# A SwiGLU down projection by seven products: sums of the activations formed by accumulating transfers instead of by VectorE

## The chip, the cores and the metric

The kernel runs on one core of a Trainium2 chip. The metric is the device time of one execution in microseconds (us). Its core has TensorE (PE in the profile; PEld is its weight load), VectorE (DVE), ScalarE (ACT), GpSimd (POOL) and SyncE (SP), which work side by side and wait for each other through semaphores, and 16 DMA engines that carry all transfers. A transfer is issued by an engine's queue, here SP's or GpSimd's; one that adds to what lies at its destination is issued by GpSimd.

## The reference

A layer of a streaming encoder over 512 positions of width 1024, in float32. The part that matters is its end, the feed-forward network, with 2816 inner channels:

```
h2 = rms_norm(x, norm_ffn[l])
act = silu(h2 @ w_ffn_gate) * (h2 @ w_ffn_up)
x = x + act @ w_ffn_down
```

## The kernel before, in words

Every matmul operand is split into a high part, rounded to the format that TensorE takes (float32r), and a low part, the rest; a product is three matmuls (high-high, low by high, high by low). Weights are split as they come: ScalarE copies the raw tile to the high part (`whd` in the down projection), VectorE subtracts to get the low part (`wld`). The weight tiles have three buffers.

The feed-forward network is computed in steps c = 0 to 10, each of which leaves a block of 256 channels, `act0` to `act10`, each 128 x 2 x 512 (its last axis is the position). `finish_act` ends a step: it adds what TensorE summed, multiplies the gate half and the up half by `rb2` (the inverse root mean square of each position), applies SiLU to the gate half and multiplies. It is called for tx and for ty, the tiles of a step's two halves of 128 channels, each with gate and up half side by side.

The down projection does `act0` directly (L1587 to L1605) and the other ten blocks by a seven-product scheme (Winograd's form of Strassen's), which replaces eight block products by seven on sums of blocks. The activations are cut in 2 x 2: inner half i (act1 to act5, act6 to act10) by position half j. A block (i, j) is named by `ablk` in three parts kh of two, two and one acts. The products run in the order

```
DORDER = ("11", "12", "S1", "S2", "S3", "S4", "22")
```

and take as activation operands: block (0,0); block (1,0); T1 = (0,0) - (0,1); T2 = -T1 - (1,1); T3 = (1,1) - (0,1); block (1,1); T4 = -T2 - (1,0). VectorE forms T1, T2 and T4 in place of block (0,0) and T3 in place of (0,1) (`in_place`, L1570), five instructions each. `split_d2` splits an operand: ScalarE writes the high part (L1400), VectorE the low part (L1401), into tiles `Bd` + the product's name + kh + h or l. So `BdS10h` is the high part of the first third of T1.

The weights of each product lie in five sets n = 0 to 4 of 512 KB. Raw sets of product 11 are `dw110` to `dw114`, of product 21 `dw210` to `dw214`; sums of weights for S1, S2 and S3 are formed in them by accumulating transfers from DRAM on GpSimd's queue (`dadd`, L1537), each issued when the set has been split. Sets of products 12 and 22 come on SP's queue into three raw buffers, `dr120` to `dr124` and `dr220` to `dr224`; the fourth load waits until the first set has been split. Each product is done for two output halves q; with `USE` the five sets follow each other once: sets 0, 1 and half of set 2 for q = 0, the other half and sets 3, 4 for q = 1. The profile leaves numbers out of names, so `whd<-dr` is any high part of a set of product 12 or 22, and `act<-act` any of the in-place sums.

What stands where between the products is written out by hand: the table `LATER` lists, for each product, calls that prepare later operands, and after each of a product's six pieces two (q = 0) or one (q = 1) of them are recorded. The order on each engine then follows from priorities of a scheduling layer, except where `keep_in_program_order` holds it. An engine does its instructions in that order, and a waiting one holds up all behind it on the same engine.

Of the kernel before, what the change touches and what calls it, by code (L numbers as in the profile page):

```python
# [8 lines left out]
F32 = mybir.dt.float32  # L9
F32R = mybir.dt.float32r  # L10
BF16 = mybir.dt.bfloat16
AF = mybir.ActivationFunctionType
ALU = mybir.AluOpType
# [18 lines left out]
H = S // 2  # L32
# [34 lines left out]
def layer_kernel(ctx: ExitStack, tc: tile.TileContext, x, xt, vecs, w_in, w_qkv7, w_gate7, w_pool, w_rg, w_ig,  # L67
                 w_branch, w_br7, w_out, w_fd, w_gu7, w_fd7, out):
    nc = tc.nc
    act = nc.scalar.activation  # L70
    dve = nc.vector
# [12 lines left out]
    def b4(shape, name, tag="b", dt=F32):  # L84
        bufs = {"w": NAW, "t": NAT, "b": NAB}[tag]
        return pools["ap0"].tile([P] + shape, dt, tag=tag, name=name, bufs=bufs)
# [317 lines left out]
    with ExitStack() as first:  # L404
# [394 lines left out]
        for t in VKQ:  # L799
            ps = {}  # L800
            r = {}
# [15 lines left out]
            for nm in ORDER:  # L817
                if nm in ("11", "12", "S1", "22"):
                    bank(nm)
                dst = {"S2": "11", "S3": "11", "S4": "S1"}.get(nm, nm)  # L820
# [28 lines left out]
        for cc in range(2):  # L849
            tx, ty = b4([2, S], f"gx{cc}"), b4([2, S], f"gy{cc}")  # L850
# [3 lines left out]
            Y = pb.tile([P, 2, S], F32, tag="mm", name=f"ps_gy{cc}")  # L854
            X = pb.tile([P, 2, S], F32, tag="mm", name=f"ps_gx{cc}")
# [8 lines left out]
            for nm in ORDER:  # L864
                ps, half, first_, t, ts_, src, ss = plan[nm]
# [314 lines left out]
    with ExitStack() as third:  # L1180
# [42 lines left out]
        for u, nm in BORDER:  # L1223
# [3 lines left out]
            ps = bank[u, z]  # L1227
            ah = weights("b7", u, nm)
            b = BH[nm]
            for w in range(2):  # L1230
                o = ps[:, w, half * H:(half + 1) * H]
# [4 lines left out]
            if sn is not None:  # L1236
                if (u, sn) not in snaps:
                    snaps[u, sn] = ap2.tile([P, 2, S], F32, tag="t", name=f"bt{u}{sn}")
                with tc.high_priority(EARLY):
                    act(snaps[u, sn][:, :, ts_], ps[:, :, hi], AF.Copy,  # L1240
                        scale=-1.0 if sn and (u, sn) in gated else 1.0)
# [10 lines left out]
    with ExitStack() as ffn:  # L1252
        gp = ffn.enter_context(tc.tile_pool(name="gp", bufs=GBUFS))

        def g4(shape, name, dt=F32):

            return gp.tile([P] + shape, dt, tag="g", name=name)

        def small(name, bufs=1, tag=None, dt=F32):
            return gp.tile([P, S], dt, tag=tag or name, name=name, bufs=bufs)  # L1260
# [3 lines left out]
        act(onesr, ones, AF.Copy)  # L1264
        sqsum = small("sqsum")
        rb2 = small("rb2")

        x1p = {}
        x1 = []

        def rms2():
            sh = small("sqh", 2, "sq2", F32R)
            sl = small("sql", 2, "sq2", F32R)
            act(sh, sqsum, AF.Copy)
            dve.tensor_tensor(sl, sqsum, sh.bitcast(F32), ALU.subtract)
            ps = fp.tile([P, 2, S], F32, tag="mm", name="ps_rms2")[:, 0, :]
            for n, t in enumerate((sh, sl)):
                tc.keep_in_program_order(nc.tensor.matmul(ps, onesr, t, start=n == 0, stop=n == 1))
            ms = small("ms2", 2, "sq2")
            t = small("rst2", 2, "sq2")  # L1280
            dve.tensor_scalar(ms, ps, 1.0 / D, EPS, ALU.mult, ALU.add)
            tc.keep_in_program_order(nc.scalar.preload_act_table_set("natural_log_exp_and_others"))
            act(t, ms, AF.Ln)
            act(t, t, AF.Exp, scale=-0.5)
            dve.tensor_tensor(rb2, t, t, ALU.mult)
            dve.tensor_tensor(rb2, rb2, ms, ALU.mult)
            dve.tensor_scalar(rb2, rb2, -0.5, 1.5, ALU.mult, ALU.add)
            dve.tensor_tensor(rb2, rb2, t, ALU.mult)

# [95 lines left out]
        def ablk(i, kh, j):  # L1387
            return [acts[1 + 5 * i + 2 * kh + n][:, :, j * H:(j + 1) * H] for n in range(2 - kh // 2)]

        def split_d2(nm, kh, i, j):  # L1390

            pin = tc.keep_in_program_order if nm not in ("11", "12") else lambda i: None
            if kh < 2:
                h, l = g4([4, H], f"Bd{nm}{kh}h", F32R), g4([4, H], f"Bd{nm}{kh}l", F32R)
            else:
                t = g4([2, 2, H], f"Bd{nm}{kh}", F32R)
                h, l = t[:, 0], t[:, 1]
            for n, src in enumerate(ablk(i, kh, j)):
                ns = slice(2 * n, 2 * n + 2)
                act(h[:, ns, :], src, AF.Copy)  # L1400
                pin(dve.tensor_tensor(l[:, ns, :], src, h[:, ns, :].bitcast(F32), ALU.subtract))  # L1401
            DB[nm, kh] = h, l

        def finish_act(t, ps, a, sign):

            dve.tensor_tensor(t, t, ps, ALU.add)
            for w in range(2):
                dve.tensor_tensor(t[:, w, :], t[:, w, :], rb2, ALU.mult)
            act(t[:, 0, :], t[:, 0, :], AF.Silu, scale=sign)
            if sign > 0:  # L1410
                dve.tensor_tensor(a, t[:, 0, :], t[:, 1, :], ALU.mult)
            else:
                dve.scalar_tensor_tensor(a, t[:, 1, :], sign, t[:, 0, :], ALU.mult, ALU.mult)


        PRE = ("S2", "S4", "22")

        def seven(n):
            c, nm = steps[n]
            lo, hi = slice(0, H), slice(H, S)  # L1420
            if nm == "11":
                acts.append(g4([2, S], f"act{c}"))
                T[c] = g4([2, S], f"tx{c}"), g4([2, S], f"ty{c}")
                Z[c] = [fp.tile([P, 2, S], F32, tag="mm", name=f"ps_{z}{c}") for z in "yx"]
            (tx, ty), (Y, X), a = T[c], Z[c], acts[c]
            make_a(n + 3)
            if c == 0:
                ps, kh = (Y, X)[CH[nm]], KH[nm]
                w = A.pop((c, nm))
                for j in range(2):  # L1430
                    product(w, B[0, f"{kh + 1}{j + 1}"], ps, j, kh == j == 0, kh == 1)
                for f in SPREAD[nm]:
                    f()
                if kh:
                    t = (tx, ty)[CH[nm]]
                    for w in range(2):
                        dve.tensor_tensor(t[:, w, :], ps[:, w, :], rb2, ALU.mult)
                    act(t[:, 0, :], t[:, 0, :], AF.Silu)
                    dve.tensor_tensor(a[:, CH[nm], :], t[:, 0, :], t[:, 1, :], ALU.mult)
                return  # L1440

            ps, half, first, t, ts_ = {"11": (Y, 1, True, tx, lo),
                                       "12": (X, 0, True, None, None),
                                       "S1": (X, 1, False, ty, hi),
                                       "S2": (Y, 1, False, tx, hi),
                                       "S4": (X, 1, False, None, None),
                                       "22": (Y, 0, False, None, None),
                                       "S3": (Y, 1, False, ty, lo)}[nm]
            product(A.pop((c, nm)), B[0, WITH[nm]], ps, half, first, True)
            if t is not None:  # L1450
                with tc.high_priority(EARLY):
                    act(t[:, :, ts_], ps[:, :, hi], AF.Copy)
            if (c, nm) == (1, "S1"):
                split_b("T3", "T3")
            if c == DOWN - 1 and nm == "S2":
                ah.extend(g4([2, S], "a" + p_, F32R) for p_ in "hl")
                act(ah[0], acts[0], AF.Copy)
                dve.tensor_tensor(ah[1], acts[0], ah[0].bitcast(F32), ALU.subtract)
            if c == DOWN - 1 and nm in PRE:
                split_d2("11", PRE.index(nm), 0, 0)  # L1460
            if nm == "S4":
                finish_act(tx, X, a[:, 0, :], 1.0)
            if nm == "S3":
                finish_act(ty, Y, a[:, 1, :], -1.0)

        T, Z, ah = {}, {}, []

# [2 lines left out]
        for c in range(4):  # L1470
# [13 lines left out]
            for j in range(2):  # L1484
# [3 lines left out]
                t = x1p[c // 2, j][:, c % 2, :]  # L1488
# [15 lines left out]
        for n in range(len(steps)):  # L1504
            seven(n)
# [6 lines left out]
        for m in range(4):  # L1512
            t = fp.tile([P, 2, S], F32, tag="mm", name=f"ps_d{m}")
# [54 lines left out]
        def in_place(dst, sign, op, other):  # L1568
            return [lambda kh=kh: [tc.keep_in_program_order(
                dve.scalar_tensor_tensor(t, t, sign, o, ALU.mult, op)) for t, o in zip(ablk(dst[0], kh, dst[1]), ablk(other[0], kh, other[1]))]  # L1570
                    for kh in range(3)]

        def both(nm, i, j):
            return [lambda kh=kh: split_d2(nm, kh, i, j) for kh in range(3)]
# [4 lines left out]
                   lambda: [dload("21", n, DX) for n in range(5)],  # L1579
                   lambda: [dadd("22", n, DX) for n in range(5)]] + both("12", 1, 0)[:1])  # L1580

        LATER = {"11": both("12", 1, 0)[1:] + in_place((0, 0), 1.0, ALU.subtract, (0, 1)) + both("S1", 0, 0),
                 "12": in_place((0, 0), -1.0, ALU.subtract, (1, 1)) + both("S2", 0, 0),
                 "S1": in_place((0, 1), -1.0, ALU.add, (1, 1)) + both("S3", 0, 1),
                 "S2": both("S4", 1, 1) + in_place((0, 0), -1.0, ALU.subtract, (1, 0)),
                 "S3": both("22", 0, 0)}

        for e in range(2):
# [48 lines left out]
        for nm in DORDER:  # L1637
            z, half, first, adds = plan[nm]
            todo = LATER.get(nm, [])
            n0 = dsets.index((nm, 0))  # L1640
            for q in range(2):
                if (nm, q) == ("22", 1):

                    make_d(len(dsets))
                    for w, ps in enumerate((XY[1, "y"], XY[0, "x"])):
# [3 lines left out]
                        t = x1p[q, 1][:, ws, lo]  # L1649
# [67 lines left out]
```

## Time and profile before

| | us |
|---|---|
| median of 3 runs | 900.3 |
| lowest, highest | 899.79, 902.87 |
| the profiled execution's own time | 900.52 |
| its span in the trace | 898.7 |
| TensorE busy | 891.1 |
| VectorE busy | 736.7 |
| ScalarE busy | 532.9 |
| GpSimd busy | 106.7 |

The span runs from the first to the last instruction; the execution's own time has 1.8 us around it.  A timeline row gives start and duration in us, engine, line, operation, what is written and read, shapes, and in brackets the idle time before it with what ended it. A row of transfers gives count, KB of each and the median time from issue to landing. The down projection by seven products begins at about 795 us of the span and ends with it.

### The profile page before, as it was taken

The page shows a single profiled execution, that of the slowest core. Times are in us where ns is not written, and L with a number is a line of the kernel's source. Part 1 is how long each engine was busy: PE and PEld are TensorE (multiplying, and loading weights), DVE is VectorE, ACT ScalarE, POOL GpSimd, SP SyncE. Part 2 cuts the span into 40 slices and gives each one's busy share as a digit, 9 for nine tenths or more (in the row PEclk, how much of TensorE's full clock was granted, in tenths as well). Part 3 has the DMA queues.
Part 4 walks back from the last instruction along what each step waited for, and adds up shares of the span by engine and source line. Part 5 has one row for each costly group of instructions (what it writes and reads, how often), then busy time and mean ns, then how long its engine had stood idle before and what let it go on. Part 6 is the DMA issues. An engine that isn't in the chain of part 4 may idle for free.

```text
span 898.7 us, 14578 instructions
## 1 busy us (share of the span) xinstructions
PE 891.1 (99%) x5731; PEld 802.4 (89%) x5731; DVE 736.7 (82%) x937; ACT 532.9 (59%) x747; POOL 106.7 (12%) x150
## 2 busy tenths in 40 slices
PE   9999999999999999999999999999999999998998
PEld 6888778888899888888888988999999999998998
DVE  7897897988786599967887685798888888998974
ACT  7554989556856556555664545655555555654642
POOL 1010002232332101000001100000010100121200
PEclk9999999999999999999999999999999999999999
DMA  9485347798582786634635864836666676887913
GB/s 342 141 309 150 114 132 210 220 299 244 179 262 71 234 234 192 218 118 145 214 93 154 190 179 164 258 81 174 169 148 176 162 169 201 211 210 205 196 39 117
DMA packets 83620, 164.59 MB, mean 183 GB/s; under 512 B 7904, under 2 KB 48864, under 8 KB 83552
## 3 DMA queue, kind: packets, MB, share of 16 engines
q1 hardware_dynamic: 68000, 107.29, 35.9%
q0 software_dynamic: 15408, 56.11, 28.2%
q8 instruction: 45, 0.74, 0.3%
q10 hardware_dynamic: 144, 0.26, 0.1%
q14 instruction: 23, 0.19, 0.1%
HBM read 143.19 MB, written 18.87 MB: 180 GB/s over the span
## 4 chain that ended last, share of the span: by engine, by line
PE 93%; DVE 3%; ACT 2%; DMA 1%; issue 1%; DVEq 0%; ACTq 0%; SPq 0%
PE ps_y L283 13%; PE ps_x L283 10%; PE ps_q L794 7%; PE ps_dy L1633 5%; PE ps_dx L1633 4%; PE ps_br L274 3%; PE ps_br L275 3%; PE ps_br L276 3%; PE ps_bY L1234 2%; PE ps_gy L283 2%; PE ps_gate L697 2%; PE ps_gate L276 2%; PE ps_bX L1234 2%; PE ps_gx L283 2%; PE ps_gate L274 2%; PE ps_gate L275 2%
## 5 line engine op out<-in xcount | busy, mean ns | idle before, releaser
L110 ACT ACTIVATE whi<-raw 128x1024 fp32r<-128x1024 f32 x61 | 64.6, 1059 | 73.3 <-PE ps_br L275 14.7
L111 DVE TENSOR_TENSOR wlo<-raw,whi 128x1024 fp32r<-128x1024 f32 x61 | 74.4, 1220 | 28.9 <-ACT whi L110 28.9
L111 DVE TENSOR_TENSOR wlo<-qw,whi 128x1024 fp32r<-128x1024 f32 x48 | 58.6, 1222 | 20.8 <-ACT whi L110 20.4
L110 ACT ACTIVATE whi<-qw 128x1024 fp32r<-128x1024 f32 x48 | 50.7, 1057 | 33.1 <-PE ps_q L794 18.7
L1379 ACT ACTIVATE wh<-w 128x1024 fp32r<-128x1024 f32 x34 | 36.2, 1064 | 49.4 <-PE ps_x L283 24.7
L1380 DVE TENSOR_TENSOR wl<-w,wh 128x1024 fp32r<-128x1024 f32 x34 | 41.6, 1223 | 7.3 <-ACT wh L1379 6.7
L1380 DVE TENSOR_TENSOR wl_S<-w,wh_S 128x1024 fp32r<-128x1024 f32 x30 | 36.6, 1220 | 12.1 <-ACT wh_S L1379 12.0
L1379 ACT ACTIVATE wh_S<-w 128x1024 fp32r<-128x1024 f32 x30 | 31.8, 1060 | 22.5 <-PE ps_y L283 19.8
L1379 ACT ACTIVATE whdS<-dw 128x1024 fp32r<-128x1024 f32 x20 | 21.3, 1064 | 22.1 <-PE ps_dy L1633 11.1
L1380 DVE TENSOR_TENSOR wldS<-dw,whdS 128x1024 fp32r<-128x1024 f32 x20 | 24.2, 1220 | 6.4 <-ACT whdS L1379 6.3
L1050 DVE TENSOR_TENSOR_SCAN E<-K,ahead 128x512 f32<-128x512 f32 (+3 forms) x32 | 25.3, 812 | 4.4 <-ACT K L1046 4.4
L274 PE MATMUL ps_br<-yHH,whi 128*128 128x512 f32 x64 | 25.3, 395 | 0.0
L274 PE MATMUL ps_lru<-HH,whi 128*128 128x512 f32 x64 | 25.2, 394 | 0.0
L274 PE MATMUL ps_br<-yph,whi 128*128 128x512 f32 x64 | 25.2, 394 | 0.0
L274 PE MATMUL ps_pool<-HH,whi 128*128 128x512 f32 x64 | 25.2, 393 | 0.0
L274 PE MATMUL ps_gate<-HH,whi 128*128 128x512 f32 x64 | 25.0, 391 | 0.0
L276 PE MATMUL ps_gate<-HH,wlo 128*128 128x512 f32 x64 | 25.0, 391 | 0.0
L275 PE MATMUL ps_br<-ypl,whi 128*128 128x512 f32 x64 | 25.0, 391 | 0.0
L276 PE MATMUL ps_br<-yph,wlo 128*128 128x512 f32 x64 | 25.0, 391 | 0.0
L275 PE MATMUL ps_br<-yHL,whi 128*128 128x512 f32 x64 | 25.0, 390 | 0.0
L276 PE MATMUL ps_br<-yHH,wlo 128*128 128x512 f32 x64 | 25.0, 390 | 0.0
L275 PE MATMUL ps_pool<-HL,whi 128*128 128x512 f32 x64 | 25.0, 390 | 0.0
(768 smaller groups left out, 3540.0 us busy)
## 6 DMA issues: line engine op xcount, KB each, us to landing
w<-in_w_gu_dram SPq DMA_DIRECT2D x44, 512.0 KB, 6.6
raw<-in_w_in_dram SPq DMA_DIRECT2D x31, 512.0 KB, 5.2
qw<-in_w_qkv_dram SPq DMA_DIRECT2D x24, 512.0 KB, 6.5
w<-in_w_gu_dram POOLq DMA_DIRECT2D x20, 512.0 KB, 7.3
dw<-in_w_down_dram POOLq DMA_DIRECT2D x20, 512.0 KB, 8.0
raw<-in_w_branch_dram SPq DMA_DIRECT2D x16, 512.0 KB, 4.2
qw<-in_w_qkv_dram POOLq DMA_DIRECT2D x12, 512.0 KB, 7.8
qd<-r POOLq DMA_DIRECT2D x12, 512.0 KB, 7.8
```

The costliest lines, as they stand in the source:

```text
L110: act(hi, raw, AF.Copy)
L111: dve.tensor_tensor(lo, raw, hi.bitcast(F32), ALU.subtract)
L274: nc.tensor.matmul(ps, lh, rh, start=start, stop=False, skip_group_check=skip)
L275: nc.tensor.matmul(ps, lh, rl, start=False, stop=False, skip_group_check=skip)
L276: nc.tensor.matmul(ps, ll, rh, start=False, stop=stop, skip_group_check=skip)
L283: nc.tensor.matmul(o, a_[a][:, w, k, :], b_[b][:, k, :], start=first and n == k == 0, stop=last and n == 2 and k == 3, skip_group_check=True)
L794: nc.tensor.matmul(ps[:, a, :], b_[:, k, ts_], a_[:, kk, :], start=first and n == k == 0, stop=n == 2 and k == 3, skip_group_check=True)
L1050: dve.tensor_tensor_scan(E[:, c0:c0 + n][:, ::-1], K[:, c0 + 1:c0 + n + 1][:, ::-1], ahead[:, S - n:][:, ::-1], 0.0, ALU.mult, ALU.add)
L1234: nc.tensor.matmul(o, ah[x_][:, w, k, :], b[k][y_], start=first_ and n == k == 0, stop=n == 2 and k == 3, skip_group_check=True)
L1379: act(h, src, AF.Copy)
L1380: dve.tensor_tensor(l, src, h.bitcast(F32), ALU.subtract)
L1633: nc.tensor.matmul(o, a_[a][:, w, k0 + k, :], b_[b][:, k, :], start=first and i == k == 0, stop=last and i == 2 and k == nk - 1, skip_grou ...
```

## The change

T1 and T2 are formed by accumulating transfers from SBUF to SBUF (`dma_sum`, ten of 128 x 2 x 256, 256 KB each) in place of block (0,0): T1 after block (0,0) has been split for product 11, T2 after T1 has been split for S1. Since a transfer can only add, block (0,1) is written negated: in steps c = 1 to 5 the up half is multiplied by `rbn`, which is `rb2` for the first 256 positions and its negative for the others (two ScalarE copies, into the tile of `sqsum`, which is no longer needed then). T1 + (1,1) is then the negative of T2, so the split for S2 writes it negated (high part with scale -1, low part by one scalar_tensor_tensor). T3 and T4 stay with VectorE, with their signs changed to match. In `LATER` the five entries of product 11 that summed and split T1 become three that split T1 and issue T2's transfers, and the sums of T2 go from the list of product 12.

```
+        rbn = sqsum
...
+            act(rbn[:, :H], rb2[:, :H], AF.Copy)
+            act(rbn[:, H:], rb2[:, H:], AF.Copy, scale=-1.0)
...
+        def dma_sum(dst, kh, other):
+            for t, o in zip(ablk(dst[0], kh, dst[1]), ablk(other[0], kh, other[1])):
+                nc.gpsimd.dma_start(t, o, accum_op=ALU.add)
+
         def split_d2(nm, kh, i, j):
...
+                if nm == "S2":
+                    act(h[:, ns, :], src, AF.Copy, scale=-1.0)
+                    pin(dve.scalar_tensor_tensor(l[:, ns, :], src, -1.0, h[:, ns, :].bitcast(F32), ALU.mult,
+                                                 ALU.subtract))
+                    continue
                 act(h[:, ns, :], src, AF.Copy)
...
-        def finish_act(t, ps, a, sign):
+        def finish_act(t, ps, a, sign, up):
...
-            for w in range(2):
-                dve.tensor_tensor(t[:, w, :], t[:, w, :], rb2, ALU.mult)
+            for w, r in enumerate((rb2, up)):
+                dve.tensor_tensor(t[:, w, :], t[:, w, :], r, ALU.mult)
...
             if c == DOWN - 1 and nm in PRE:
                 split_d2("11", PRE.index(nm), 0, 0)
+                dma_sum((0, 0), PRE.index(nm), (0, 1))
             if nm == "S4":
-                finish_act(tx, X, a[:, 0, :], 1.0)
+                finish_act(tx, X, a[:, 0, :], 1.0, rbn if c < 6 else rb2)
...
-        LATER = {"11": both("12", 1, 0)[1:] + in_place((0, 0), 1.0, ALU.subtract, (0, 1)) + both("S1", 0, 0),
-                 "12": in_place((0, 0), -1.0, ALU.subtract, (1, 1)) + both("S2", 0, 0),
-                 "S1": in_place((0, 1), -1.0, ALU.add, (1, 1)) + both("S3", 0, 1),
-                 "S2": both("S4", 1, 1) + in_place((0, 0), -1.0, ALU.subtract, (1, 0)),
+        LATER = {"11": both("12", 1, 0)[1:] + [lambda kh=kh: (split_d2("S1", kh, 0, 0), dma_sum((0, 0), kh, (1, 1)))
+                                               for kh in range(3)],
+                 "12": both("S2", 0, 0),
+                 "S1": in_place((0, 1), 1.0, ALU.add, (1, 1)) + both("S3", 0, 1),
+                 "S2": both("S4", 1, 1) + in_place((0, 0), 1.0, ALU.subtract, (1, 0)),
```

The order moves at three places. Lines of the changed kernel are 4 to 15 higher than those of the kernel before.

GpSimd's queue at the start of the down projection, before, from the accumulating transfer into set 0 of product 11 (`dw110`) to that into set 4 (`dw114`):

```order
L1537 DMA dw110_8043<-in_w_down7_dram 128x1024
L1537 DMA dw212_8057<-in_w_down7_dram 128x1024
L1537 DMA dw111_8045<-in_w_down7_dram 128x1024
L1537 DMA dw112_8047<-in_w_down7_dram 128x1024
L1537 DMA dw113_8049<-in_w_down7_dram 128x1024
L1537 DMA dw114_8051<-in_w_down7_dram 128x1024
```

The same piece of the changed kernel (`act1` to `act5` on the left are the blocks summed into):

```order
L1551 DMA dw110_8050<-in_w_down7_dram 128x1024
L1396 DMA act5_6671<-act5_6671 128x2x256
L1551 DMA dw212_8064<-in_w_down7_dram 128x1024
L1551 DMA dw111_8052<-in_w_down7_dram 128x1024
L1551 DMA dw112_8054<-in_w_down7_dram 128x1024
L1551 DMA dw113_8056<-in_w_down7_dram 128x1024
L1396 DMA act1_5755<-act6_6899 128x2x256
L1396 DMA act2_5987<-act7_7127 128x2x256
L1396 DMA act3_6215<-act8_7355 128x2x256
L1396 DMA act4_6443<-act9_7583 128x2x256
L1551 DMA dw114_8058<-in_w_down7_dram 128x1024
L1396 DMA act5_6671<-act10_7802 128x2x256
```

The fifth sum of T1 (`act5<-act5`) and all five of T2 have come in between; T1's other four stand a little above this piece, among the accumulating transfers into `dw211` to `dw214`.

ScalarE in the same stretch, before, from the last split of T1 (`BdS12`; `BdS20h` is the first of T2):

```order
L1400 ACTIVATE BdS12_8292<-act5_6669 128x512
L1379 ACTIVATE whd122_8326<-dr122_8266 128x1024
L1379 ACTIVATE whd123_8360<-dr123_8299 128x1024
L1400 ACTIVATE BdS20h_8389<-act1_5753 128x512
L1400 ACTIVATE BdS20h_8389<-act2_5985 128x512
L1379 ACTIVATE whd124_8395<-dr124_8330 128x1024
```

And in the changed kernel:

```order
L1413 ACTIVATE BdS12_8255<-act5_6671 128x512
L1383 ACTIVATE whd120_8272<-dr120_8194 128x1024
L1383 ACTIVATE whd121_8302<-dr121_8241 128x1024
L1409 ACTIVATE BdS20h_8363<-act1_5755 128x512
L1409 ACTIVATE BdS20h_8363<-act2_5987 128x512
L1383 ACTIVATE whd122_8333<-dr122_8276 128x1024
L1409 ACTIVATE BdS21h_8369<-act3_6215 128x512
L1409 ACTIVATE BdS21h_8369<-act4_6443 128x512
L1383 ACTIVATE whd123_8375<-dr123_8306 128x1024
L1409 ACTIVATE BdS22_8403<-act5_6671 128x512
L1383 ACTIVATE whd124_8406<-dr124_8337 128x1024
```

The splits have moved up against the weight copies of product 12: `BdS12` stood behind `whd120` and `whd121` and stands ahead of them, and T2's splits stand ahead of `whd122`, `whd123` and `whd124`.

VectorE, before, from the sums of T1 (L1570) to the low part of set 0 of product 12 (`wld120`):

```order
L1570 SCALAR_TENSOR_TENSOR act4_6441<-act4_6441 128x2x256
L1380 TENSOR_TENSOR wld114_8218<-dw114_8051,whd114_8217 128x1024
L1570 SCALAR_TENSOR_TENSOR act5_6669<-act5_6669 128x2x256
L1401 TENSOR_TENSOR BdS10l_8238<-act1_5753,BdS10h_8237 128x512
L1401 TENSOR_TENSOR BdS10l_8238<-act2_5985,BdS10h_8237 128x512
L1624 TENSOR_TENSOR x100_5274<-x100_5274,ps_dy0_8140 128x2x256
L1401 TENSOR_TENSOR BdS11l_8257<-act3_6213,BdS11h_8256 128x512
L1401 TENSOR_TENSOR BdS11l_8257<-act4_6441,BdS11h_8256 128x512
L1380 TENSOR_TENSOR wld120_8263<-dr120_8187,whd120_8262 128x1024
```

And in the changed kernel:

```order
L1414 TENSOR_TENSOR BdS10l_8221<-act1_5755,BdS10h_8220 128x512
L1414 TENSOR_TENSOR BdS10l_8221<-act2_5987,BdS10h_8220 128x512
L1414 TENSOR_TENSOR BdS11l_8229<-act3_6215,BdS11h_8228 128x512
L1414 TENSOR_TENSOR BdS11l_8229<-act4_6443,BdS11h_8228 128x512
L1384 TENSOR_TENSOR wld114_8237<-dw114_8058,whd114_8236 128x1024
L1414 TENSOR_TENSOR BdS12_8255<-act5_6671,BdS12_8255 128x512
L1639 TENSOR_TENSOR x100_5274<-x100_5274,ps_dy0_8147 128x2x256
L1384 TENSOR_TENSOR wld120_8273<-dr120_8194,whd120_8272 128x1024
```

The sums of T1 are gone (three more stood above the first piece), and the low part of `BdS12` has come ahead of `wld120`.

More of the change, by code (lines that the diff above doesn't have):

```diff
@@ L1460, in seven @@
                 split_d2("11", PRE.index(nm), 0, 0)
+                dma_sum((0, 0), PRE.index(nm), (0, 1))
             if nm == "S4":
-                finish_act(tx, X, a[:, 0, :], 1.0)
+                finish_act(tx, X, a[:, 0, :], 1.0, rbn if c < 6 else rb2)
             if nm == "S3":
-                finish_act(ty, Y, a[:, 1, :], -1.0)
+                finish_act(ty, Y, a[:, 1, :], -1.0, rbn if c < 6 else rb2)
         T, Z, ah = {}, {}, []
```

## The prediction

> **What bounds the kernel now.** The page comes first: where is the time, and which engine has none to spare?
>
> ```profile
> span 898.7 us, 14578 instructions
> PE 891.1 (99%) x5731; PEld 802.4 (89%) x5731; DVE 736.7 (82%) x937; ACT 532.9 (59%) x747; POOL 106.7 (12%) x150
> PE 93%; DVE 3%; ACT 2%; DMA 1%; issue 1%; DVEq 0%; ACTq 0%; SPq 0%
> ```
>
> TensorE is busy for 99% of the span. The change removes no matmul, so it can win or lose only where TensorE waits or runs at a lower clock. The table by stretches of 5 us at the start of the down projection shows where that is. Its columns are the stretch and its length, busy time of PE, PEld, DVE, ACT and POOL, the granted clock, the DMA engines' share and GB/s.
>
> ```profile
> 785.00:790.00 5.00, 5.00 (x24) 4.14 (x23) 5.00 (x7) 3.22 (x6) 1.87 (x3) 1.00 1.03 331
> 790.00:795.00 5.00, 5.00 (x26) 4.18 (x25) 4.95 (x9) 1.42 (x3) 0.00 (x0) 1.00 1.05 272
> 795.00:800.00 5.00, 5.00 (x45) 5.00 (x44) 5.00 (x8) 3.06 (x4) 0.00 (x0) 1.00 0.77 170
> 800.00:805.00 5.00, 5.00 (x45) 5.00 (x44) 5.00 (x7) 3.73 (x6) 3.43 (x4) 1.00 0.56 83
> 805.00:810.00 5.00, 4.14 (x37) 3.95 (x36) 5.00 (x9) 3.21 (x5) 0.85 (x1) 1.00 1.06 207
> 810.00:815.00 5.00, 5.00 (x44) 5.00 (x45) 5.00 (x7) 0.00 (x0) 0.00 (x0) 1.00 1.07 230
> 815.00:820.00 5.00, 3.68 (x31) 3.27 (x29) 1.90 (x3) 2.10 (x3) 0.00 (x0) 1.00 0.91 319
> 820.00:825.00 5.00, 4.76 (x27) 4.76 (x28) 5.00 (x9) 4.01 (x6) 0.00 (x0) 0.66 0.51 151
> ```
>
> TensorE loses 0.86 us in 805:810, 1.32 in 815:820, 0.24 in 820:825, and in the last stretch the clock stands at 0.66, which is another 0.34 x 5 = 1.7 us of work: 4.1 us in all. VectorE is full from 785 to 815. The DMA engines are full (1.03 to 1.07) in two stretches, with slack between 795 and 805. The chain of waits there says what ended those losses.
>
> ```profile
> 808.84 1.15 DVE wld L1380
> 810.04 7.72 DMA dr<-in_w_down_dram
> 817.87 1.07 ACT whd L1379
> 818.96 1.24 DVE wld L1380
> 820.24 19.80 PE ps_dx L1633 x158
> ```
>
> The low part of weight set 0 of product 12 (wld120) is ready at 810.0, 0.86 us after TensorE wanted it. It also frees the buffer for set 3, whose load lands 7.72 us later, at 817.8; that ends the second wait. T1 on VectorE stands ahead of wld120, so taking it off is aimed at both.
>
> **The change, part by part.** VectorE's instructions and ScalarE's:
>
> ```profile
> L1570 DVE SCALAR_TENSOR_TENSOR act<-act 128x512 f32<-128x512 f32 x5 | 3.2, 683 | 0.0
> L1380 DVE TENSOR_TENSOR wld<-dr,whd 128x1024 fp32r<-128x1024 f32 x5 | 6.1, 1217 | 3.1 <-ACT whd L1379 3.1
> L1379 ACT ACTIVATE whd<-dr 128x1024 fp32r<-128x1024 f32 x5 | 5.3, 1059 | 10.0 <-DMA dr<-in_w_down_dram 8.3 <-issue 1.1 <-ACT BdS11h L1400 0.6
> L1400 ACT ACTIVATE BdS20h<-act 128x512 fp32r<-128x512 f32 x2 | 1.1, 615 | 0.0
> ```
>
> *Removed:* ten VectorE sums, five for T1 and five for T2, at 683 ns each or about 0.6 start to start. Of T1 five lay ahead of wld120: 3.0 us. One split (BdS12) is moved ahead of it: 0.6. So by VectorE alone wld120 would come 2.4 us earlier, at 807.6.
>
> *Added early:* two ScalarE copies of half a tile, once, before the table load of the first SiLU. They fit:
>
> ```profile
> 588.94 1.28 ACT L1438 ACT_TABLE_LOAD   x1
> 591.57 0.63 ACT L1438 ACTIVATE tx<-tx 128x512 f32<-128x512 f32 x1 [1.35 <-DVE tx L1437]
> ```
>
> ScalarE idles 1.35 us there for VectorE; two copies at less than 0.62 each fit, and TensorE waits for nothing near. I cost them at nothing; uncovered, they would cost 1.2. The negated copy and the other signs change no count.
>
> *Added, and what decides:* ten transfers of 256 KB on GpSimd's queue. Their places are in the pieces of the order shown with the change. On GpSimd T1's first four sums stand above the piece, the fifth at its head; T2's first four stand behind four weight adds (dw212, dw111, dw112, dw113), its fifth behind one more (dw114). On ScalarE the split BdS12 now stands ahead of whd120, which it followed before, and BdS20 (two rows), BdS21 (two) and BdS22 stand ahead of whd122, whd123 and whd124; before, whd122 and whd123 came first.
>
> T2's splits (BdS2), not wanted by TensorE until product S2, now stand ahead of three weight copies that it wants in product 12. Each split waits for its sum to land. So whd122 waits for T2's second sum, whd123 for its fourth, whd124 for its fifth, and VectorE's low parts and TensorE behind them. On GpSimd the new waits are for T1's splits; behind them stand only adds that products S2 and S3 want later.
>
> When do those land? How GpSimd's queue drains, first its issues, then times to landing of single issues, picked by their time: the last before 800 (from 786.6), the first, fourth and fifth after it (from 800.67, 803.4, 805.53), one alone (826.60), and of SP's the load that GpSimd waits for (784.64), outputs of 256 KB and of 512 KB (each 256 rows, of 1 and of 2 KB), and the page's row of SP's queue with packets, MB and share.
>
> ```profile
> 800.67 3.57 POOL L1537 DMA_DIRECT2D dw<-in_w_down_dram  x4 [12.86 <-DMA dw<-in_w_down_dram]
> 805.53 0.85 POOL L1537 DMA_DIRECT2D dw<-in_w_down_dram  x1 [1.29 <-DVE wld L1380]
> dw<-in_w_down_dram POOLq DMA_DIRECT2D x1, 512.0 KB, 13.7
> dw<-in_w_down_dram POOLq DMA_DIRECT2D x1, 512.0 KB, 5.5
> dw<-in_w_down_dram POOLq DMA_DIRECT2D x1, 512.0 KB, 10.4
> dw<-in_w_down_dram POOLq DMA_DIRECT2D x1, 512.0 KB, 12.1
> dw<-in_w_down_dram POOLq DMA_DIRECT2D x1, 512.0 KB, 5.4
> dw<-in_w_down_dram SPq DMA_DIRECT2D x1, 512.0 KB, 15.5
> out_dram<-x SPq DMA_DIRECT2D x2, 256.0 KB, 2.2
> out_dram<-x SPq DMA_DIRECT2D x1, 512.0 KB, 2.8
> q1 hardware_dynamic: 68000, 107.29, 35.9%
> ```
>
> Landings on the queue: 800.3; then 806.2 and, three adds later, 813.8, which is 2.5 us an add, whatever the spacing of the issues; then 817.6. They drain one after the other. What a sum of 256 KB takes there no row shows. By its bytes it is half an add, 1.27 us; by its 256 rows (an add has 128) two adds, 5.1. Of the outputs with equal rows the one of half the bytes lands in 2.2 us instead of 2.8, so rows are not all that counts; I stay nearer to the bytes and take 1.5.
>
> The sum, with the queue full from 800.3 on (before, it was empty there until the load of 784.64 had landed at 800.1): T1's five end at 800.3 + 5 x 1.5 = 807.8. ScalarE's BdS12 (0.6) and whd120 (1.06) and VectorE's wld120 (1.2) follow: 810.7, no earlier than the 810.0 of before, so the aimed gain is gone. Four weight adds: + 10.1 = 817.9. The loads of sets 3 and 4 of product 12 go out at about 810 and share the engines; by the page's row a load of 0.52 MB takes 0.359 x 898.7 x 0.52 / 107.29 = 1.6, both 3.1, and I put them ahead of T2's sums. T2's sums land at 822.5, 824.0, 825.5 and 827.0, the fifth after one more add at 831.0. Then split 0.6, copy 1.06, low part 1.2: set 2 is whole at 826.9, set 3 at 830.5 (VectorE does four splits between), set 4 at 833.9. What TensorE did before at these places:
>
> ```profile
> 815.52 0.28 PE L1633 MATMUL ps_dx<-Bd,whd 128*128 128x256 f32 x1
> 824.46 0.28 PE L1633 MATMUL ps_dx<-Bd121h,whd 128*128 128x256 f32 x1
> ```
>
> Set 2 was begun at 815.52 and set 4 at 824.46. Now TensorE stands from about 815 to 826, does sets 2 and 3 as they come, and begins set 4 at 833.7, or at 834.0 if the clock halves after the long wait as it did above. 834.0 - 824.5 = 9.5 us later. The 4.1 us lost before are inside this difference and not to be subtracted again. From there on both engines have the same order as before, so the shift stays. The profiled execution took 900.5 (median 900.3): 900.5 + 9.5 = **910.0**.
>
> T1's sums also meet the loads on SP's queue between 785 and 800. GpSimd's queue held adds all that time, so the loads' share changes little; if they came later, set 2 of product 11 would be late first, but the queue's times, on which the end hangs, stay.
>
> A rule speaks otherwise. The Trainium skill, page "DMA: Bandwidth & Descriptors", section "Anatomy of one DMA — SWDGE (gpsimd) path", fits a transfer from GpSimd as 2.0 us plus its bytes over 436 GB/s, 2.6 us for such a sum (an estimate from that page), and the sum would be rival B's by it. The trace disagrees: an add alone takes 5.4 us, and 12.1 in the queue.
>
> **The rivals.**
> *A, the rows are dear.* A sum takes as long as an add, 2.5 us. Ten sums stand ahead of set 4, each 1.0 longer: 920. For it: rows of 1 KB, and both ends in SBUF. Against: the 2.2 us of the outputs.
> *B, the sums do not queue (faster).* Each lands about 4.1 us after its issue (5.4 less half an add). T2's second is issued at about 805 and lands at 809; whd122 is wanted at 815.5 less the first wait, 814.7, so nothing waits. wld120 at 807.6 ends the first wait (0.86), the load of set 3 lands at 815.3 and leaves 0.4 of the second, and the clock stays up: 0.86 + 1.2 + 1.7 = 3.8 less: 896.7. It decides if T2's fifth lands before 821. Against it: the landings above.
> *C, no change.* T1's sums fit in the queue's idle time between 800.3 and the adds' start, the loads cost nothing: T2's second lands at 816.3, its fifth at about 822.6, set 4 is begun 0.8 later: 901.3.
>
> **How the numbers follow.** Forecast 0.67, A 0.18, B 0.07, C 0.08. Within the forecast: sums at 1.27 take off 2.3, loads that do not lie ahead 3.1: down to 904.6. The upper end goes to A's 920; 904 leaves out B and C, 0.15. Less than 0.3% (2.7 us) is what a measurement cannot tell from no change: faster 0.07, same 0.06, slower 0.87.
>
> **What would show it.** Right: ScalarE idle for about 10 us before BdS20h, released by a transfer act<-act; TensorE idle once from about 815 to 826; VectorE's 20 sums down to 10; the wait at 810 still there. Wrong: sums landing within 5 us of issue, whd122 done by 815, or TensorE's wait at whd120 growing (T1's sums dearer than thought) instead of at whd122.

## The result, and the profile after

The changed kernel takes 909.66 us (median of 6 runs, 908.36 to 911.47); the kernel before, run beside it on the same chip, 902.79 (899.79 to 902.87). The ratio is 1.0087, with a 95% interval of 1.0069 to 1.0105: slower by 6.2 to 9.5 us. A ratio here is taken over all runs, so it is not quite that of the two medians, which lie 6.9 apart. The profiled executions lie 9.0 apart (909.51 against 900.52), and so do the spans. The forecast was 910.0, in a range of 904 to 920.

The page of the changed kernel, the rows that answer to those of before:

```profile
span 907.7 us, 14597 instructions
PE 892.6 (98%) x5731; PEld 803.7 (89%) x5731; DVE 731.1 (81%) x927; ACT 533.5 (59%) x749; POOL 118.8 (13%) x160
PE 91%; DVE 3%; DMA 2%; ACT 2%; issue 1%; POOL 0%; SPq 0%; DVEq 0%; ACTq 0%; POOLq 0%
```

VectorE has ten instructions and 5.6 us less to do, and the span is 9.0 us longer. In the chain the share of DMA has gone from 1% to 2%, that of PE from 93% to 91%. The stretches of 5 us around the place, with the columns as before:

```profile
805.00:810.00 5.00, 4.55 (x38) 4.15 (x36) 2.23 (x4) 2.53 (x3) 2.91 (x3) 1.00 1.11 213
810.00:815.00 5.00, 4.42 (x38) 4.42 (x39) 2.26 (x3) 0.00 (x0) 2.05 (x2) 1.00 1.06 217
815.00:820.00 5.00, 1.09 (x10) 0.89 (x8) 0.00 (x0) 0.00 (x0) 0.00 (x0) 1.00 1.09 291
820.00:825.00 5.00, 0.68 (x2) 0.50 (x2) 0.70 (x1) 2.72 (x4) 0.00 (x0) 0.58 1.22 205
825.00:830.00 5.00, 4.54 (x21) 4.42 (x21) 4.10 (x7) 2.27 (x4) 0.00 (x0) 0.50 0.86 208
```

From 815 to 820 ScalarE, VectorE and GpSimd do nothing, TensorE 1.09 us; only the DMA engines are full. What TensorE and VectorE wait for is seen on ScalarE, in order of time (in brackets the idle time and what ended it):

```profile
807.43 0.63 ACT L1413 ACTIVATE BdS<-act 128x512 fp32r<-128x512 f32 x1 [4.57 <-DMA act<-act]
807.97 1.99 ACT L1383 ACTIVATE whd<-dr 128x1024 fp32r<-128x1024 f32 x2
821.36 0.63 ACT L1409 ACTIVATE BdS20h<-act 128x512 fp32r<-128x512 f32 x1 [11.40 <-DMA act<-act]
822.69 0.63 ACT L1409 ACTIVATE BdS20h<-act 128x512 fp32r<-128x512 f32 x1 [0.70 <-DMA act<-act]
823.23 1.04 ACT L1383 ACTIVATE whd<-dr 128x1024 fp32r<-128x1024 f32 x1
824.17 0.61 ACT L1409 ACTIVATE BdS21h<-act 128x512 fp32r<-128x512 f32 x1
825.53 0.63 ACT L1409 ACTIVATE BdS21h<-act 128x512 fp32r<-128x512 f32 x1 [0.74 <-DMA act<-act]
826.07 1.04 ACT L1383 ACTIVATE whd<-dr 128x1024 fp32r<-128x1024 f32 x1
829.31 0.63 ACT L1409 ACTIVATE BdS<-act 128x512 fp32r<-128x512 f32 x1 [2.20 <-DMA act<-act]
```

The first row is the copy of T1's last third, the later ones are T2's. Each row that a transfer released starts within some hundredths of a microsecond of its landing, so this list is also the list of landings: T1's fifth sum at 807.4; T2's first, second, fourth and fifth at 821.3, 822.7, 825.5 and 829.3. Behind them come the copies `whd122` (823.23), which TensorE has wanted since 816, and `whd123` (826.07). The chain of work there:

```profile
804.18 18.49 DMA act<-act
823.23 1.05 ACT whd L1383
824.30 1.24 DVE wld L1384
825.58 19.49 PE ps_dx L1648 x147
```

A sum of 256 KB, T2's second, is issued at 804.18 and lands 18.49 us later; a copy and a low part follow, and TensorE goes on, at half clock (0.50 in 825 to 830). Its first matmuls of set 2 and of set 4 of product 12 in the timeline:

```profile
824.32 0.80 PE L1648 MATMUL ps_dx<-Bd,whd 128*128 128x256 f32 x2 [8.23 <-ACT whd L1383]
833.46 0.28 PE L1648 MATMUL ps_dx<-Bd121h,whd 128*128 128x256 f32 x1
```

TensorE has waited 8.23 us. It begins set 4 at 833.46, against 824.46 before: 9.00 us, which is the whole difference of the spans.

### The profile page after: what moved, and what is told of

It is laid out like the page before. It is cut to its first block, busy times and chain, and to the rows that moved or that the text cites. A ratio compares the mean times of both kernels' runs of the same rounds, so it can differ in the third digit from the quotient of the medians.

```text
span 907.7 us, 14597 instructions
## 1 busy us (share of the span) xinstructions
PE 892.6 (98%) x5731; PEld 803.7 (89%) x5731; DVE 731.1 (81%) x927; ACT 533.5 (59%) x749; POOL 118.8 (13%) x160
## 4 chain that ended last, share of the span: by engine, by line
PE 91%; DVE 3%; DMA 2%; ACT 2%; issue 1%; POOL 0%; SPq 0%; DVEq 0%; ACTq 0%; POOLq 0%
PE ps_y L283 13%; PE ps_x L283 10%; PE ps_q L794 7%; PE ps_dx L1648 5%; PE ps_dy L1648 4%; PE ps_br L274 3%; PE ps_br L275 3%; PE ps_br L276 3%; PE ps_gate L697 2%; PE ps_bY L1234 2%; PE ps_gy L283 2%; DMA act<-act 2%; PE ps_gate L276 2%; PE ps_bX L1234 2%; PE ps_gx L283 2%; PE ps_gate L274 2%
## 5 line engine op out<-in xcount | busy, mean ns | idle before, releaser
L1384 DVE TENSOR_TENSOR wld<-dr,whd 128x1024 fp32r<-128x1024 f32 x10 | 12.1, 1222 | 17.0 <-ACT whd L1383 17.0
L1551 POOL DMA_DIRECT2D dw<-in_w_down_dram x20 | 17.7, 945 | 60.1 <-DVE wldS L1384 33.7
```

The lines of the kernel that those rows point to most:

```text
L1384: dve.tensor_tensor(l, src, h.bitcast(F32), ALU.subtract)
```

## The experiments

Three theories are told apart. **Q**: the loss comes from when T2 is ready. Its sums stand in GpSimd's queue behind weight adds, and ScalarE meets T2's copies ahead of product 12's weight copies. **W**: ten sums are that much more work for the transfer engines, which are full there, wherever the sums stand. **O**: the order on ScalarE alone is at fault, whoever forms the sums. Each kernel is the changed one with the edit shown; each ratio is to runs of the kernel before on the same chip, and the us behind it are the ratio's. Line numbers shift by a few from kernel to kernel, the names of tiles stay. `issue_after` puts what is recorded under it behind the given instruction on that instruction's engine.

### One half of the change at a time

T1 alone:

```
-        LATER = {"11": both("12", 1, 0)[1:] + [lambda kh=kh: (split_d2("S1", kh, 0, 0), dma_sum((0, 0), kh, (1, 1)))
-                                               for kh in range(3)],
-                 "12": both("S2", 0, 0),
+        LATER = {"11": both("12", 1, 0)[1:] + both("S1", 0, 0),
+                 "12": in_place((0, 0), 1.0, ALU.add, (1, 1)) + both("S2", 0, 0),
```

> Only T1's five sums are transfers; T2 is formed in place by VectorE again, with its block still written negated. Theory Q (the loss comes from T2's five sums, which land late because GpSimd's queue works in order behind the weight adds, and which ScalarE meets with T2's copies standing ahead of product 12's weight copies): T2's sums on VectorE are ready within some us of T1's copies, so TensorE's 8 us wait at product 12 goes, and T1's sums in their late place in the queue leave the wait at wld120 about as it was: within 2 us of before. Theory W (ten sums are that much more work for the transfer engines, and every load and add pays for it): half of the sums, half of the loss, 4 to 5 us above before. Theory O (the order in which the copies of T2 are recorded is at fault, whoever forms the sums): the copies are recorded as in the change, so the loss stays, 7 to 9 us above before.

T2 alone:

```
-                dma_sum((0, 0), PRE.index(nm), (0, 1))
...
+        LATER = {"11": both("12", 1, 0)[1:] + in_place((0, 0), 1.0, ALU.add, (0, 1))
+                 + [lambda kh=kh: (split_d2("S1", kh, 0, 0), dma_sum((0, 0), kh, (1, 1))) for kh in range(3)],
```

> Only T2's five sums are transfers; T1 is formed in place by VectorE, as an addition, since its second block is written negated. GpSimd's queue has all five weight adds of product 11 ahead of T2's sums, and ScalarE has T2's copies ahead of product 12's last two weight copies instead of its last three. Theory Q: T2's sums stand behind the adds as in the change, though 6 to 7 us of T1's sums are gone from the queue; so T2's first lands at 816 to 819 and a wait of 3 to 6 us at product 12 stays: 3 to 7 us above before, most of the loss of the change. Theory W: five sums as in the run with T1 alone, so the same 2.5 us above before as that one.

T1 alone: 903.57 against 900.29, ratio 1.0028 (1.0012 to 1.0043), 2.5 us. T2 alone: 910.20 against 900.45, ratio 1.0104 (1.0083 to 1.0125), 9.4 us. TensorE's waits from 785 to 880, of T1 alone and then of T2 alone (behind the colon: us in total, how many, the longest):

```profile
PE ps_dx L1647 <- DVE wld L1384: 2.5, 3, 1.0
PE ps_dx L1647 <- ACT whd L1383: 1.1, 2, 0.9
```

```profile
PE ps_dx L1647 <- ACT whd L1383: 9.2, 2, 8.3
PE ps_dx L1647 <- DVE wld L1384: 0.5, 1, 0.5
```

The long wait belongs to T2. W asked for two equal halves, and falls with that. T1's 2.5 us is a little more than Q allowed. T2's 9.4 is well above the 3 to 7 that I expected: five sums are gone from the queue, and T2's first still landed at 822.9. GpSimd's waits from 780 to 835 in that run say why:

```profile
POOL dw L1550 <- DMA dw<-in_w_down_dram: 12.5, 1, 12.5
```

GpSimd stood 12.5 us, until 801.96, in front of one add (`dw212`) whose own load had not landed; then four adds went out at once. The next kernel is this one with that add behind T2's sums.

### The add at the head of the queue

```
-                   lambda: [dadd("22", n, DX) for n in range(5)]] + both("12", 1, 0)[:1])
+                   lambda: [dadd("22", n, DX) for n in (0, 1, 3, 4)]] + both("12", 1, 0)[:1])
...
+        def add222():
+            with tc.issue_after(last[0].ins):
+                dadd("22", 2, DX)
...
-                 "12": both("S2", 0, 0),
+                 "12": [add222] + both("S2", 0, 0),
```

`last[0]` is the last of T2's sums.

> The run with T2 alone lost as much as the change, though its queue carries five sums fewer. Its trace has GpSimd waiting 12.5 us, to 801.96, for the load of the third of product S1's raw tiles, with four more adds behind that one. Here the add into that tile stands behind T2's sums, and nothing else of the run with T2 alone is moved. If the head of the queue is what held it (theory Q, with the cause of the miss named so), the other four adds are issued from about 797 to 807 and land by 813, T2's first sum lands at 814 to 816 instead of 822.9, the last at 820 to 822 instead of 830.0, and the time is 2 to 5 us above before. If the adds and sums cost that much wherever they stand, or the copies of T2 on ScalarE alone do it, it stays 8 to 10 us above before.

904.98 against 903.21, ratio 1.0029 (1.0009 to 1.0050), 2.6 us: most of the 9.4 us went with the place of one add. How much is not sharp: by the ratios it is 6.8, but the kernel before was 2.8 us slower beside this run than beside the run with T2 alone, and the two medians of the edited kernels are 5.2 apart. TensorE's waits there:

```profile
PE ps_dx L1653 <- ACT whd L1383: 3.9, 2, 3.1
PE ps_dx L1653 <- DVE wld L1384: 1.2, 2, 0.8
```

ScalarE's copies of T2 in the timeline:

```profile
816.80 0.63 ACT L1415 ACTIVATE BdS20h<-act 128x512 fp32r<-128x512 f32 x1 [4.56 <-DMA act<-act]
818.72 0.63 ACT L1415 ACTIVATE BdS20h<-act 128x512 fp32r<-128x512 f32 x1 [1.29 <-DMA act<-act]
821.91 0.63 ACT L1415 ACTIVATE BdS21h<-act 128x512 fp32r<-128x512 f32 x1 [1.60 <-DMA act<-act]
825.85 0.63 ACT L1415 ACTIVATE BdS21h<-act 128x512 fp32r<-128x512 f32 x1 [3.31 <-DMA act<-act]
828.54 0.63 ACT L1415 ACTIVATE BdS<-act 128x512 fp32r<-128x512 f32 x1 [1.12 <-DMA act<-act]
```

The first sum lands at 816.8, 6 us earlier than without the edit, though not as early as expected; the last at 828.5, where I expected 820 to 822. The sums come 1.9, 3.2, 3.9 and 2.7 us apart, where the changed kernel had them 1.4 apart. In this run they share the engines with SP's loads for product 12 and 22 (issued from 812.5 on); in the changed kernel the loads of product 12 had landed by then.

### The sums by VectorE, in the change's order

```
-                nc.gpsimd.dma_start(t, o, accum_op=ALU.add)
+                tc.keep_in_program_order(dve.tensor_tensor(t, t, o, ALU.add))
```

> The change with its order of recording, but the ten sums are VectorE additions (128x512 each) where the change records the ten transfers; T2's copies stand on ScalarE ahead of product 12's second weight copy, earlier than in the change. Theory Q: what hurts is only when T2 is ready; on VectorE that is before 812, so no 8 us wait; VectorE's ten additions of about 0.7 us stand among product 11's last weight splits instead, so 0 to 3 us above before. Theory O: the copies are ahead of the weight copies, 7 to 9 us above before. Theory W: no transfer is added, so as before.

901.00 against 900.29, ratio 1.0012 (0.9999 to 1.0026), 1.1 us. TensorE's waits:

```profile
PE ps_dy L1648 <- DVE wld L1384: 2.1, 1, 2.1
PE ps_dx L1648 <- DVE wld L1384: 0.2, 1, 0.2
```

T2's first copies stand ahead of `whd121` here, one place earlier than in the change, and nothing in product 12 waits more than 0.2 us: T2 is ready when they come. The order by itself costs nothing, so O falls. The 2.1 us is a new wait, in product 11 (`ps_dy`, until 800.94), for a low part that VectorE begins at 799.67. Sums of T1 stand ahead of it, the last at 795.47; that they are what delays it was not tested by itself.

### Each cause taken away

The weight adds that follow product 11 behind T2's sums:

```
+        def add21():
+            for ns, i in ((range(2), last[0]), (range(2, 5), AI["11"])):
+                with tc.issue_after(i.ins):
+                    for n in ns:
+                        dadd("21", n, DY)
...
-                if nm in NEXT:
+                if nm in NEXT and nm != "11":
...
+                 "S2": [add21] + both("S4", 1, 1) + in_place((0, 0), 1.0, ALU.subtract, (1, 0)),
```

`AI["11"]` is the last of the five adds that follow product S1's splits, into its set 4.

> The change, with the five weight adds that follow product 11 (the second block into product 11's tiles, wanted for product S3 only) issued behind T2's five sums: two of them right behind, three behind the next adds of product S1's tiles. Nothing else is moved, and ScalarE still has T2's copies ahead of product 12's weight copies, there ahead of its second one. Theory Q: T2's first sum is issued at about 802 instead of 802.9, but has at most one add and T1's last sum ahead of it, so the first lands at about 808 to 810 instead of 821, the last at about 814 to 816 instead of 829, TensorE's 8 us wait at product 12 goes, and the kernel ends 4 us below before to 1 us above it. Theory W: the same number of sums and adds, so the loss stays or shrinks little, 5 to 9 us above before. Theory O: T2's copies are still ahead of the weight copies, so 5 to 9 us above before.

T2's copies behind product 12's weight copies:

```
-                    act(h[:, ns, :], src, AF.Copy, scale=-1.0)
+                    tc.keep_in_program_order(act(h[:, ns, :], src, AF.Copy, scale=-1.0))
...
-                 "12": both("S2", 0, 0),
-                 "S1": in_place((0, 1), 1.0, ALU.add, (1, 1)) + both("S3", 0, 1),
+                 "12": [lambda: None] * 3,
+                 "S1": both("S2", 0, 0) + in_place((0, 1), 1.0, ALU.add, (1, 1)) + both("S3", 0, 1),
```

> The change, with T2's copies (the splits for product S2) recorded one product later and held in that place on ScalarE, so that all of product 12's weight copies stand ahead of them; GpSimd's queue is as in the change, and T2's sums land as late as there (last at about 829). Theory Q: nothing of product 12 waits for T2 any more, TensorE's 8 us wait goes; what is left is the weight adds of product S1 and S2, which stand behind T2's sums in the queue, 1 to 2 us: 1 us below before to 3 us above it. Theory W: loads and adds are as late as in the change, so 5 to 9 us above before. Theory O says as Q here.

The adds behind: 902.95 against 900.29, ratio 1.0029 (1.0015 to 1.0043), 2.6 us. The copies behind: 904.93 against 900.29, ratio 1.0051 (1.0029 to 1.0072), 4.6 us. Either edit takes the 8 us wait away, though neither comes as near to before as Q had it (up to 1 and up to 3 us above), and 4.6 is close to W's 5 to 9, so the second run alone does not tell Q from W. With the adds behind, what TensorE and ScalarE waited for:

```profile
PE ps_dx L1658 <- ACT whd L1383: 2.4, 1, 2.4
ACT whd L1383 <- DMA dr<-in_w_down_dram: 6.1, 1, 6.1
```

The loads of sets 3 and 4 of product 12 in that run, picked by their issue at 808.3 and 813.2:

```profile
dr<-in_w_down_dram SPq DMA_DIRECT2D x1, 512.0 KB, 6.0
dr<-in_w_down_dram SPq DMA_DIRECT2D x1, 512.0 KB, 9.4
```

T2's sums landed from 809.0 to 816.0, as expected. What is late next is set 4 of product 12: its buffer comes free only after `whd121`, which still stands behind a copy of T2, and the load lands at 822.7. With the copies behind, ScalarE's longest wait for a transfer, and the waits of TensorE:

```profile
ACT BdS L1413 <- DMA act<-act: 5.1, 1, 5.1
...
PE ps_dx L1648 <- ACT whd L1383: 1.8, 1, 1.8
PE ps_dy L1648 <- DVE wldS L1384: 1.2, 2, 0.8
PE ps_dx L1648 <- DVE wld L1384: 1.0, 1, 1.0
```

Here it is T1's last sum, which lands at 810.3 and holds `whd120`. TensorE waits 2.8 us for it (1.8 and 1.0), against 0.9 at that place before, and the granted clock is 0.5 to 0.7 from 812 to 820. Why this sum lands 2.9 us later than in the change is not shown.

### Both causes taken away, and T1 as well

Both edits together:

> The run with the weight adds behind T2's sums, and T2's copies behind product 12's weight copies on ScalarE besides. In the run with the adds alone moved the fourth and fifth raw tile of product 12 were late (issued at 808.3 and 813.2, landed at 814.3 and 822.7), the fifth since its place comes free only when the second weight copy is done, which stood behind a copy of T2. Theory Q: with that gone the fifth load is issued by 809.5 and lands by 817 to 819, TensorE's wait there shrinks from 2.4 us to under 1: 2 us below before to 1 us above it. Theory W (the transfer engines are full here, their share is over 1.0 from 785 to 820): the fifth tile lands at 821 or later whenever it is issued, and the time is that of the run with the adds alone moved, 2 to 4 us above before.

With T1's sums ahead of the five adds of product S1 besides:

```
-                   lambda: [dadd("22", n, DX) for n in range(5)]] + both("12", 1, 0)[:1])
+                   add22] + both("12", 1, 0)[:1])
```

`add22` issues the same five adds behind T1's last sum.

> The run before this one with T1's five sums ahead of all five adds into product S1's tiles too, so that GpSimd's queue has T1's sums, S1's adds, T2's sums, two adds of S3, S2's adds, three of S3. Theory Q: T1's last sum lands when it can be issued at 790 with four sums ahead of it, at about 797 to 799 instead of 805 to 807, so wld120 waits for nothing; but S1's five adds now stand between T1's and T2's, and T2's first lands later by about 8 us, which costs nothing with T2's copies behind: 3 us below before to 1 us above it. If instead the load of the fifth raw tile is the bound (Theory W), 2 to 4 us above before.

And both edits with T1 by VectorE, so that only T2's five sums are transfers:

> T1 in place by VectorE as in the run with T2 alone; T2's sums by transfers, ahead of the weight adds after product 11, and T2's copies behind product 12's weight copies. GpSimd's queue carries five sums instead of ten. Theory Q: no wait on T2; T1's wait at wld120 is that of before (0.9 us): 2 us below before to 1 us above it. Theory W: five more sums than before, so 1 to 3 us above it.

| | ratio to before | TensorE's waits, 785 to 880 | T1's fifth sum lands | T2's second, fifth |
|---|---|---|---|---|
| before | 1 | 2.5 | | |
| the change | 1.0087 | 9.7 | 807.4 | 822.7, 829.3 |
| both behind | 0.9985 (0.9968 to 1.0003) | 0.8 | 804.6 | 809.8, 818.6 |
| and T1 first | 0.9991 (0.9976 to 1.0006) | 2.6 | 795.1 | 811.7, 821.4 |
| T2 only, both behind | 1.0001 (0.9987 to 1.0015) | 1.7 | | 813.5, 824.7 |

Medians: 899.91, 900.07 and 901.01, all against 900.45. With both behind, the stretches where the change lost its time, columns as before:

```profile
810.00:815.00 5.00, 5.00 (x47) 5.00 (x46) 1.23 (x1) 0.15 (x2) 0.40 (x1) 1.00 1.10 254
815.00:820.00 5.00, 5.00 (x45) 4.92 (x44) 2.56 (x3) 2.99 (x4) 0.00 (x0) 1.00 1.08 273
820.00:825.00 5.00, 5.00 (x47) 5.00 (x46) 3.46 (x4) 3.35 (x5) 1.68 (x2) 1.00 1.04 306
```

And all that TensorE waited for from 785 to 880:

```profile
PE ps_dy L1658 <- DVE wldS L1384: 0.8, 1, 0.8
```

All ten sums are still there, with the DMA engines full (1.04 to 1.10), and TensorE does not wait in product 12 at all. The load of set 4 goes out at 809 and lands at 817.5, inside the 817 to 819 that Q expected. So ten sums by transfer cost no more here than by VectorE (0.9968 to 1.0003), and W falls a second time. That T1's sums go first brings the fifth's landing 9.5 us forward (to 795.1, expected 797 to 799) but does not move the time: by then nothing waits for T1.

None of the three is shown to be faster than the kernel before. The best trace (897.02 us, the fastest of that kernel's 12 runs) has 0.8 us of waits left; the median is 899.91 and the interval includes 1. What the sums on VectorE had cost before is at most a few tenths of a per cent.

## Why the prediction was right

**The place and the mechanism.** ScalarE idled 11.4 us before `BdS20h`, released by a transfer; TensorE stood once, from about 816 to 824 (forecast 815 to 826); the wait at 810 was still there (0.45 + 0.58 us, 0.86 before); VectorE's sums went from 20 to 10. All four had been named. The runs show that it takes two things together: T2 late, and its copies ahead of the weight copies. Take the one or the other away and 2.6 or 4.6 us remain; take both away and none does.

**The queue, term by term.** T1's fifth sum: forecast 807.8, landed 807.4. The forecast for T2's second, fourth and fifth was 824.0, 827.0 and 831.0; they landed at 822.7, 825.5 and 829.3. The four weight adds and the two loads put ahead of T2's sums were priced at 13.2 us, with T2's first sum 14.7; from T1's fifth to T2's first it took 13.9. A sum, priced at 1.5 us between bounds of 1.27 and 5.1, took 1.3 to 1.4. Set 4 of product 12: forecast 834.0, begun 833.46. The shift was forecast as 9.5 us and is 9.0; the rest of the program carried it on unchanged.

**Where the sum was lucky.** In the forecast set 4 is begun when T2's fifth sum has been split and its weights are ready, and half clock adds 0.3 us. In the run the low parts of sets 3 and 4 were ready earlier than that:

```profile
827.85 1.22 DVE L1384 TENSOR_TENSOR wld<-dr,whd 128x1024 fp32r<-128x1024 f32 x1
830.92 1.23 DVE L1384 TENSOR_TENSOR wld<-dr,whd 128x1024 fp32r<-128x1024 f32 x1 [0.25 <-ACT whd L1383]
```

Set 4 was whole at 832.15 (forecast 833.9), but TensorE, which had no more waits there, came to it only at 833.46, since it did set 2 and part of set 3 at half clock. At the pace of set 0 (2.6 us from its third matmul to the next set) it would have gone through sets 2 and 3 by 831.7 and waited for set 4 until 832.2. By that estimate about 1.5 of the 9.0 us is the clock, five times the forecast's 0.3, and sums that landed 1.3 to 1.7 us earlier than forecast made up for it. The queue and the order were right; that the total came within half a microsecond is in part chance.

**What hides at no cost.** The two copies into `rbn`:

```profile
589.01 0.40 ACT L1291 ACTIVATE sqsum<-rb 128x256 f32<-128x256 f32 x1
589.32 0.40 ACT L1292 ACTIVATE sqsum<-rb 128x256 f32<-128x256 f32 x1
589.74 1.28 ACT L1451 ACT_TABLE_LOAD   x1
591.75 0.63 ACT L1451 ACTIVATE tx<-tx 128x512 f32<-128x512 f32 x1 [0.73 <-DVE tx L1450]
```

ScalarE still waits for VectorE at the end, 0.73 us instead of 1.35: covered, as forecast.

**The rivals.** A (the rows are dear, 920) falls by the 1.4 us between landings. C (no change) falls by the landings behind the adds: T2's second at 822.7, not 816.3. B (the sums do not queue, 896.7) falls in this kernel: one landed 18.49 us after its issue. Its price for a sum by itself, 4.1 us, was good. With only T2's sums as transfers and the queue empty, the first one, issued at 807.4:

```profile
act<-act POOLq DMA_DIRECT2D x1, 256.0 KB, 3.8
```

The Trainium skill's fit for a transfer from GpSimd (page "DMA: Bandwidth & Descriptors", section "Anatomy of one DMA — SWDGE (gpsimd) path") gives 2.6 us for it, an estimate from that page: the traces have 3.8 with the queue empty and, in the changed kernel, up to 18.5 behind other transfers.

**What the prediction did not see.** It took the four weight adds as fixed ahead of T2. Their issue hung on the load that one of them adds to; in the change that load landed at 796.1, before at 800.1, which the prediction noted only as the cause of an idle queue. With T2 alone this head of the queue set the time.

## What to carry to other kernels

A transfer that replaces an instruction is not priced by its own length but by what stands ahead of it in its queue, by what that waits for, and by who waits behind its consumer. Before moving work to such a queue, list for each landing the first instruction of another engine that stands behind its reader: here a copy wanted two products later held up a copy wanted at once. With both orders put right the transfers cost nothing that shows here. Little was to be gained by them either: VectorE was full where T1 was formed, but TensorE had waited only 2.5 us from 785 to 880 for all of that.

## What the runs showed of the hardware

Sums of 256 KB from SBUF to SBUF land 1.3 to 1.4 us apart when GpSimd's queue has the engines to itself (the changed kernel, 821.3 to 825.5), and 1.9 to 3.9 us apart beside SP's loads (T2 alone, one add behind).

The granted clock after a wait does not follow from the length of the wait alone. In the kernel before, TensorE waited 0.81 us until 818.98 and 0.76 until 820.24, and the clock stood at 0.66 from 820 to 825. With T1's sums first it waited 1.00 us until 818.18 and 0.76 until 819.44, and the clock stayed up:

```profile
815.00:820.00 5.00, 3.24 (x26) 2.84 (x25) 1.23 (x1) 1.97 (x2) 0.00 (x0) 1.00 1.12 306
820.00:825.00 5.00, 5.00 (x46) 5.00 (x45) 3.59 (x3) 2.28 (x4) 1.07 (x2) 1.00 1.06 243
```

With T1 alone TensorE lost 2.5 us from 820 to 830, and the clock stayed at 1.00 too. So a loss of 1.6 to 2.5 us can cost about 2 us more or nothing. This goes with the spread among runs of one kernel: of the 29 runs of the kernel before beside the run with both behind, the six with a mean granted clock of 0.998 or less took 902.4 to 906.5 us, the other 23 899.0 to 903.1. What decides it in a given run stays open. The Trainium skill, page "TensorE: Matmul & The Clock Gate", section "What's actually happening", has the clock fall to half after at least one idle window of about 3.4 us, and says that the window runs freely. The kernel before does not agree with the first: its clock fell after two waits of 0.8 us each. Where in such a window a wait lay is seen in no trace here, so the second can neither be confirmed nor ruled out.
